# Split weights at a new place within their buffers for each feature-major projection: a float32 decoder kernel on one Trainium2 core

## The chip, the cores and the metric

The kernel runs on one core of one Trainium2 chip. The metric is the device time of one execution in microseconds (us). The engines are named as the profile names them: PE is TensorE's matmul side and PEld its weight load, DVE is VectorE, ACT is ScalarE, POOL is GpSimd, SP is SyncE, which here only issues DMAs. SBUF is the on-chip memory in which each of 128 partitions holds its own row of bytes; PSUM is where matmuls accumulate.

## What is computed

The reference is a two-layer decoder over 256 positions of width 2048, in float32. Cut to its matrix products:

```python
# layer 0
z = rmsnorm(x, g_mix[0]) @ w_in_a[0]            # 2048 x 3584
x = x + concat([gating(z), memory_attention(z_q, mem)]) @ w_out[0]
x = x + conv_ffn(rmsnorm(x, g_ffn[0]), w_ffn_up[0], w_ffn_down[0])
# layer 1
kv = rmsnorm(x, g_kv) @ w_kv_a                  # 2048 x 576
z = rmsnorm(x, g_mix[1]) @ w_in_b[0]            # 2048 x 1024
x = x + concat([latent_attention(z, kv), memory_attention(z_q, mem)]) @ w_out[1]
x = x + conv_ffn(rmsnorm(x, g_ffn[1]), w_ffn_up[1], w_ffn_down[1])
out = rmsnorm(x, g_final)
```

`conv_ffn` is `(silu(gate) * val) @ w_down` with `[gate, val] = conv3(h @ w_up)`; `w_up` is 2048 x 11264 and `w_down` 5632 x 2048, so the two feed-forward blocks hold most of the work. `memory_attention` also projects 256 memory tokens with `w_mem_kv` (2048 x 1024 in each layer).

## The kernel before, in words

Every weight is read once from HBM and used once, for 256 positions. To keep float32 accuracy, weights and activations are each split into a high and a low part of type float32r (a rounded float32 of 4 bytes), and a product is made of three parts: high by high, high by low, low by high.

**Weights.** `chunk` (L92) fetches one piece of a weight matrix, normally 128 x 1024 floats (512 KB), with a DMA that SP issues into a buffer `raw` (L98). ACT rounds it into `whi` (L117, or L122 where a gain is multiplied in), and DVE subtracts to get `wlo` (L118, or L123). Each of `raw`, `whi` and `wlo` has four buffers of 4096 bytes in a partition. In the compiled program they follow one another without a gap; every one of the twelve starts at a byte that is 96 modulo 256.

**Feature-major projections.** `gemm_fm` (L158) makes 512 columns of the output (`nblk` = 4 blocks of 128) or 256 (`nblk` = 2). The weights are the stationary operand: each matmul first loads 128 columns of `whi` or `wlo` (512 bytes in a partition) and then streams the activation. An activation operand is `[high 256 | low 256]`, so one matmul with `whi` streams 512 columns (L140, a "high" matmul below), and one with `wlo` streams the 256 high columns (L144, a "low" matmul). `mm_fm` (L135) issues the high and the low matmuls of two chunks in runs, and turns the order round at every second call, so that runs of 32 high and 32 low matmuls come about. The results are evicted by `join` (L220) and the code of each stage. The calls with `nblk` = 4, in the program's order, are: the keys of the memory of layer 0 and of layer 1; in layer 0 four groups of `w_in_a`, four of `w_out`, 22 of `w_ffn_up` and 12 of `w_ffn_down`; in layer 1 the latent key, the latent query and the memory query, four of `w_out` and 22 of `w_ffn_up`. That is 73 calls. `keys` (L809) calls `gemm_fm` with `nblk` = 2; `queries` (L795) and the rotary key (L764 to L766) call `chunk` and `mm_fm` themselves.

**Token-major projections.** `gemm_tm` (L187) has the activations stationary and streams 512 columns of weights: `whi` (L182), `wlo` (L183) and `whi` once more (L184). It makes the values of the memory in both layers, three groups of `w_in_a`, the values of the latent attention, and the down projection of layer 1.

**Order.** The instructions' order on each engine comes from a planner that is given the program; only a stretch of the last projection is written out by hand. A buffer's next use waits until its last reader is done: `whi` for the matmuls of four chunks earlier, `raw` for DVE, and the DMA for `raw`.

Of the kernel before, what the change touches and what calls it, by code (L numbers as in the profile page):

```python
# [9 lines left out]
F32R = mybir.dt.float32r  # L10
# [6 lines left out]
P = 128  # L17
# [13 lines left out]
THETA = 10000.0  # L31
EPS = 1e-6
FF_GROUPS = (4, 4, 3)


def exact_pieces(value, bits, count):
# [33 lines left out]
class Kernel:  # L70
    def __init__(self, ctx, tc, t, out):
        self.tc, self.nc, self.t, self.out = tc, tc.nc, t, out
        self.ctx = ctx
        self.n = 0
        pool = lambda name, bufs=1, **k: ctx.enter_context(tc.tile_pool(name=name, bufs=bufs, **k))
        self.cp = pool("cp")
        self.wp = pool("wp")
        self.ap = pool("ap")
        self.ps = pool("ps", 8, space=bass.MemoryType.PSUM)
# [12 lines left out]
    def chunk(self, src, nk, ncol, gains=None, twice=False, heads=None):  # L92
        nc, n = self.nc, nk * ncol
        raw = self.wp.tile([P, 1024], F32, tag="raw", name=self.uid("raw"), bufs=4)
        hi = self.wp.tile([P, 1024], F32R, tag="whi", name=self.uid("whi"), bufs=4)
        lo = self.wp.tile([P, 1024], F32R, tag="wlo", name=self.uid("wlo"), bufs=4)
        view = lambda x: x[:, :n].rearrange("p (k c) -> p k c", k=nk)
        nc.sync.dma_start(out=view(raw), in_=src)  # L98
        if twice:
            both = lambda x: x.rearrange("p (k o c) -> p k o c", o=2, c=ncol)  # L100
            for k in range(nk):
                s = slice(k * ncol, (k + 1) * ncol)
                for o in range(2):
                    h = both(hi)[:, k, o, :]
                    nc.scalar.activation(h, raw[:, s], AF.Copy, scale=gains[k])
                    nc.vector.scalar_tensor_tensor(both(lo)[:, k, o, :], raw[:, s], gains[k], h.bitcast(F32), ALU.mult, ALU.subtract)
            return tuple(x.rearrange("p (k c) -> p k c", k=nk) for x in (hi, lo))
        if heads is not None:

            s = view(raw).rearrange("p k (h c) -> p k h c", h=2)  # L110
            for c0, c1 in ((0, heads), (heads, ncol // 2)):
                o = lambda x: view(x)[:, :, 2 * c0 : 2 * c1].rearrange("p k (h c) -> p k h c", h=2)
                nc.scalar.activation(o(hi), s[:, :, :, c0:c1], AF.Copy)
                nc.vector.tensor_tensor(o(lo), s[:, :, :, c0:c1], o(hi).bitcast(F32), ALU.subtract)
            return view(hi), view(lo)
        if gains is None:
            nc.scalar.activation(hi[:, :n], raw[:, :n], AF.Copy)  # L117
            nc.vector.tensor_tensor(lo[:, :n], raw[:, :n], hi[:, :n].bitcast(F32), ALU.subtract)  # L118
        else:
            for k in range(nk):  # L120
                s = slice(k * ncol, (k + 1) * ncol)
                nc.scalar.activation(hi[:, s], raw[:, s], AF.Copy, scale=gains[k])  # L122
                nc.vector.scalar_tensor_tensor(  # L123
                    lo[:, s], raw[:, s], gains[k], hi[:, s].bitcast(F32), ALU.mult, ALU.subtract
                )
        return view(hi), view(lo)
# [29 lines left out]
            low(jobs)  # L156

    def gemm_fm(self, src, kbs, nblk, rhs, evict, nk=2, gain=None, hooks={}):  # L158
        accs = [self.psum() for _ in range(nblk)]
        chunks = list(range(0, len(kbs), nk))  # L160
        for c0 in range(0, len(chunks), 2):
            jobs = []
            for c in chunks[c0 : c0 + 2]:
                g = None if gain is None else [gain(kbs[c + i]) for i in range(nk)]
                hi, lo = self.chunk(src(kbs[c], nk), nk, nblk * P, g)
                for b in range(nblk):
                    cols = slice(b * P, (b + 1) * P)
                    for i in range(nk):
                        kk = c + i
                        jobs.append((accs[b], hi[:, i, cols], lo[:, i, cols], rhs(kbs[kk]), kk == 0, kk == len(kbs) - 1))  # L170
            self.mm_fm(jobs, (c0 // 2) % 2)
            for c in range(c0, min(c0 + 2, len(chunks))):
                for f in hooks.get(c, ()):
                    f()
        for b in range(nblk):
            evict(b, accs[b])
# [154 lines left out]
    def gain(self, name, k):  # L331
        c = self.g[name] + k
        return self.gT[:, c : c + 1]
# [224 lines left out]
    def ffn(self, l, after=None, to_tokens=None, tokens=None):  # L558
# [5 lines left out]
        with self.tc.tile_pool(name=self.uid("ff"), bufs=1) as fp:  # L564
            g0 = 0
            for part, ng in enumerate(FF_GROUPS):
                h = self.ap.tile([P, NB, 512], F32R, tag="big", name=self.uid("h"))
# [11 lines left out]
                for g in range(g0, g0 + ng):  # L579
# [15 lines left out]
                    self.gemm_fm(self.rows(up, FF + g * 512, 512), ks, 4, lambda k: xhl[:, k, :], ev, hooks=turns)  # L595
                last = part == len(FF_GROUPS) - 1
                if last and l == 0:
# [403 lines left out]
```

## Time and profile before

| | |
|---|---|
| median of 3 runs | 2127.53 us (2127.27 to 2128.79) |
| profiled execution, first to last instruction (span) | 2125.1 us |
| instructions | 31077 |
| mean granted TensorE clock | 0.998 |
| read from HBM | 387.88 MB, 184 GB/s over the span |
| time between issue and landing of a 512 KB weight DMA | about 4.2 us |

The page gives no time for the profiled execution other than its span; the median of the runs is 2.4 us longer than it. In the profile a matmul's or a weight load's duration is modelled and contains a fixed latency, and consecutive ones overlap, so their pace is read from starts, or from the length of a run of them divided by their number.

### The profile page before, as it was taken

Reading aid. Unit: us, or ns where it says so; the run is one execution under the profiler, and the core shown is the slowest. Engines: PE = TensorE matmul, PEld = TensorE weight load, DVE = VectorE, ACT = ScalarE, POOL = GpSimd, SP = SyncE. Lnnn points to the kernel's source line nnn. Section 1 sums busy time; section 2 is a strip of 40 time slices with the busy share of each in tenths; the row PEclk is TensorE's granted clock in tenths of the full one; section 3 lists DMA queues with packets and bytes.
Section 4 is the critical chain, followed back from the end, with each engine's and each line's share of the span. In section 5 each row is a group of like instructions: output and inputs, shape, how many; then the busy total and the mean of one; then the engine's idle time right before and its main releaser. Section 6 shows DMA issues by size and latency. Waiting matters only on the chain.

```text
span 2125.1 us, 31077 instructions
## 1 busy us (share of the span) xinstructions
PE 2101.5 (99%) x11624; PEld 1831.1 (86%) x11624; DVE 1465.7 (69%) x2186; ACT 1148.7 (54%) x1773; POOL 392.8 (18%) x378
## 2 busy tenths in 40 slices
PE   8999999999999999999999999999999999999998
PEld 7888888888888888888888788888888888888886
DVE  6655667777756777567798766677775577745775
ACT  7654654556535555356556554466553555535554
POOL 1000123312101121011254111332120121201210
PEclk9999999999999999999999999999999999999999
DMA  8565555666566665666655533665656666656664
GB/s 272 178 202 178 159 187 189 189 189 191 189 194 187 185 195 188 197 182 188 192 181 165 171 114 110 196 190 170 191 196 195 187 190 190 194 195 188 189 188 149
DMA packets 207548, 392.01 MB, mean 184 GB/s; under 512 B 14302, under 2 KB 22820, under 8 KB 207268
## 3 DMA queue, kind: packets, MB, share of 16 engines
q1 hardware_dynamic: 207252, 389.50, 59.3%
q8 instruction: 91, 1.49, 0.3%
q14 instruction: 61, 0.50, 0.1%
q10 hardware_dynamic: 144, 0.52, 0.1%
HBM read 387.88 MB, written 2.10 MB: 184 GB/s over the span
## 4 chain that ended last, share of the span: by engine, by line
PE 97%; DVE 1%; ACT 1%; DMA 1%; issue 0%; SPq 0%; DVEq 0%; ACTq 0%
PE ps L140 50%; PE ps L144 26%; PE ps L182 6%; PE ps L184 6%; PE ps L183 6%; PE ps L831 1%; DMA raw<-in_w_mem_kv 0%; PE ps L829 0%; PE ps L523 0%; PE ps L488 0%; DVE wlo L118 0%; PE ps L665 0%; PE ps L852 0%; DMA raw<-in_w_in_a 0%; PE ps L393 0%
## 5 line engine op out<-in xcount | busy, mean ns | idle before, releaser
L118 DVE TENSOR_TENSOR wlo<-raw,whi 128x1024 fp32r<-128x1024 f32 x660 | 843.1, 1288 | 490.3 <-ACT whi L117 362.4
L117 ACT ACTIVATE whi<-raw 128x1024 fp32r<-128x1024 f32 x660 | 697.2, 1058 | 702.7 <-PE ps L140 525.4
L140 PE MATMUL ps<-xhl,whi 128*128 128x512 f32 x3280 | 768.9, 390 | 0.0
L140 PEld LDWEIGHTS ps<-xhl,whi 128*128 128x128 f32 x3280 | 608.6, 188 | 121.7
L571 POOL TENSOR_TENSOR a<-js,rbc 128x256 f32<-128x256 f32 x176 | 230.5, 1323 | 1101.7 <-DVE js L224 1005.8
L144 PEld LDWEIGHTS ps<-xhl,wlo 128*128 128x128 f32 x3280 | 408.7, 192 | 9.2 <-DVE wlo L118 0.6
L144 PE MATMUL ps<-xhl,wlo 128*128 128x256 f32 x3280 | 413.4, 283 | 0.4 <-DVE wlo L118 0.4
L140 PE MATMUL ps<-h,whi 128*128 128x512 f32 x704 | 164.8, 390 | 0.0
L574 ACT ACTIVATE c<-a,cT 128x256 f32<-128x256 f32 x176 | 105.2, 598 | 96.9 <-POOL a L571 95.3
L140 PEld LDWEIGHTS ps<-h,whi 128*128 128x128 f32 x704 | 130.6, 188 | 26.0
L183 PE MATMUL ps<-wlo,h 128*128 128x512 f32 x352 | 136.8, 389 | 0.0
L182 PE MATMUL ps<-whi,h 128*128 128x512 f32 x352 | 136.6, 389 | 0.0
L184 PE MATMUL ps<-whi,h 128*128 128x512 f32 x352 | 136.3, 389 | 0.0
L140 PE MATMUL ps<-mainhl,whi 128*128 128x512 f32 x512 | 119.7, 390 | 0.0
L140 PEld LDWEIGHTS ps<-mainhl,whi 128*128 128x128 f32 x512 | 95.1, 188 | 19.1
L123 DVE SCALAR_TENSOR_TENSOR wlo<-raw,gT,whi 128x512 fp32r<-128x512 f32 x112 | 87.9, 829 | 25.2 <-ACT whi L122 23.0
L576 DVE SCALAR_TENSOR_TENSOR c<-a,cT,c 128x254 f32<-128x254 f32 x176 | 101.1, 587 | 0.0
L575 DVE SCALAR_TENSOR_TENSOR c<-a,cT,c 128x255 f32<-128x255 f32 x176 | 91.6, 539 | 11.6 <-ACT c L574 11.4
L122 ACT ACTIVATE whi<-raw,gT 128x512 fp32r<-128x512 f32 x112 | 74.7, 716 | 42.3 <-PE ps L140 20.0
L224 DVE TENSOR_TENSOR js<-ps,cr 128x256 f32<-128x256 f32 x213 | 84.1, 417 | 12.6 <-POOL a L571 12.3
L222 ACT ACTIVATE cr<-ps 128x256 f32<-128x256 f32 x243 | 79.4, 373 | 19.7 <-PE ps L140 16.5
L144 PEld LDWEIGHTS ps<-h,wlo 128*128 128x128 f32 x704 | 87.7, 191 | 2.0
(248 smaller groups left out, 1856.2 us busy)
## 6 DMA issues: line engine op xcount, KB each, us to landing
raw<-in_w_ffn_up SPq DMA_DIRECT2D x352, 512.0 KB, 4.2
raw<-in_w_ffn_down SPq DMA_DIRECT2D x176, 512.0 KB, 4.4
raw<-in_w_out SPq DMA_DIRECT2D x64, 512.0 KB, 4.1
raw<-in_w_in_a SPq DMA_DIRECT2D x56, 512.0 KB, 4.1
raw<-in_w_mem_kv SPq DMA_DIRECT2D x32, 512.0 KB, 4.8
raw<-in_w_in_b SPq DMA_DIRECT2D x16, 512.0 KB, 3.9
raw<-in_w_uq SPq DMA_DIRECT2D x12, 384.0 KB, 3.3
raw<-in_w_kv_a SPq DMA_DIRECT2D x8, 512.0 KB, 4.2
```

Of the source, the lines that this page charges most:

```text
L117: nc.scalar.activation(hi[:, :n], raw[:, :n], AF.Copy)
L118: nc.vector.tensor_tensor(lo[:, :n], raw[:, :n], hi[:, :n].bitcast(F32), ALU.subtract)
L123: nc.vector.scalar_tensor_tensor(lo[:, s], raw[:, s], gains[k], hi[:, s].bitcast(F32), ALU.mult, ALU.subtract)
L140: mm(acc[:, :], wh, x, start=first, stop=last)
L144: mm(acc[:, S:], wl, x[:, :S], start=False, stop=False)
L182: mm(acc, xh, wh, start=first, stop=False)
L183: mm(acc, xh, wl, start=False, stop=False)
L184: mm(acc, xl, wh, start=False, stop=last)
L571: nc.gpsimd.tensor_tensor(a, self.join(acc), rb, ALU.mult)
L574: nc.scalar.activation(c, a, AF.Identity, scale=w(2), bias=w(3))
L575: nc.vector.scalar_tensor_tensor(c[:, 1:], a[:, : S - 1], w(1), c[:, 1:], ALU.mult, ALU.add)
L576: nc.vector.scalar_tensor_tensor(c[:, 2:], a[:, : S - 2], w(0), c[:, 2:], ALU.mult, ALU.add)
```

## The change

`hi` and `lo` become windows of 1024 floats in buffers that are 64 floats (256 bytes) longer. A counter `place` gives the start of the window. It starts at 0 and goes up by one at each call of `gemm_fm` with `nblk` = 4, modulo 64. All other users of `chunk` take the place that the counter has at that time. `raw` stays where it is in its buffer. To make room, 12 KB of a reserve at the start of SBUF, which is kept for DMA descriptors that software writes, are given up. The new buffers are 4352 bytes, and all other tiles move by multiples of 256 bytes, so place p puts a weight's start at byte (96 + 4p) modulo 256, and everything else keeps its address modulo 256.

```diff
+PLACES = 64
...
+        self.place = 0
...
-        hi = self.wp.tile([P, 1024], F32R, tag="whi", name=self.uid("whi"), bufs=4)
-        lo = self.wp.tile([P, 1024], F32R, tag="wlo", name=self.uid("wlo"), bufs=4)
+        hi = self.wp.tile([P, 1024 + PLACES], F32R, tag="whi", name=self.uid("whi"), bufs=4)
+        lo = self.wp.tile([P, 1024 + PLACES], F32R, tag="wlo", name=self.uid("wlo"), bufs=4)
+        hi, lo = (x[:, self.place : self.place + 1024] for x in (hi, lo))
...
     def gemm_fm(self, src, kbs, nblk, rhs, evict, nk=2, gain=None, hooks={}):
+        if nblk == 4:
+            self.place = (self.place + 1) % PLACES
...
-    nc = bacc.Bacc("TRN2", target_bir_lowering=False, num_devices=1)
+    nc = bacc.Bacc("TRN2", target_bir_lowering=False, num_devices=1, dynamic_dma_scratch_size=4096)
```

Counting the 73 calls gives the place of each stage: 1 and 2 for the memory's keys (and with them its values), 2 for the token-major groups of `w_in_a`, 3 to 6 for the other groups of `w_in_a`, 7 to 10 for `w_out`, 11 to 44 for the feed-forward block of layer 0 (its down projection at 19 to 22, 31 to 34 and 41 to 44), 45 to 47 for the projections of layer 1 (the rotary key at 46; values, queries and keys at 47), 48 to 51 for `w_out`, 52 to 63 and 0 to 9 for the up projections of layer 1. The three parts of its down projection, which is token-major, lie at 59, 3 and 9.

## The prediction

> **What bounds the kernel now.** I read the page first: busy times, the 40 slices, the chain of work that ended last.
>
> ```profile
> PE 2101.5 (99%) x11624; PEld 1831.1 (86%) x11624; DVE 1465.7 (69%) x2186; ACT 1148.7 (54%) x1773; POOL 392.8 (18%) x378
> ...
> PE   8999999999999999999999999999999999999998
> ...
> PEclk9999999999999999999999999999999999999999
> ```
>
> ```profile
> PE 97%; DVE 1%; ACT 1%; DMA 1%; issue 0%; SPq 0%; DVEq 0%; ACTq 0%
> ```
>
> PE is busy in every slice at the full clock, and 97% of the chain that sets the end is PE. Busy time alone can't say whether PE runs at its pace, since its durations are modelled. So next comes the chain in order of time, in a window inside the first feed-forward block (start, length, what):
>
> ```profile
> 399.90 0.36 PE ps L144 x3
> 400.26 7.28 PE ps L140 x32
> 407.54 3.83 PE ps L144 x32
> 411.38 7.28 PE ps L140 x32
> 418.66 3.83 PE ps L144 x32
> 422.49 0.69 PE ps L140 x3
> ```
>
> Each run starts where the one before ends: there is no gap. A high matmul (512 columns) takes 7.28 / 32 = 227.5 ns, a low one (256 columns) 3.83 / 32 = 119.7 ns. The difference, 107.8 ns for 256 columns, gives 0.421 ns a column, so either kind has a fixed 119.7 - 107.8 = 11.9 ns beside its columns. The same chain in the token-major down projection of layer 1:
>
> ```profile
> 1584.88 0.23 PE ps L183
> 1585.10 0.23 PE ps L184
> ...
> 1586.92 0.23 PE ps L183
> ```
>
> Nine matmuls lie between the first start and the last: 2.04 / 9 = 226.7 ns. How many there are says the view of busy time by stretch, taken over the whole span for L140, L144, L182, L183 and L184 in turn; its bracketed counts are matmuls and weight loads:
>
> ```profile
> 0.00:2126.00 2126.00, 1118.07 (x4744) 880.18 (x4744) 1.00 0.60 184
> 0.00:2126.00 2126.00, 598.33 (x4744) 591.98 (x4744) 1.00 0.60 184
> 0.00:2126.00 2126.00, 210.04 (x536) 101.11 (x536) 1.00 0.60 184
> 0.00:2126.00 2126.00, 209.22 (x536) 101.20 (x536) 1.00 0.60 184
> 0.00:2126.00 2126.00, 208.83 (x536) 101.03 (x536) 1.00 0.60 184
> ```
>
> 4744 x 0.2275 + 4744 x 0.1197 + 1608 x 0.2267 = 1079 + 568 + 365 = 2012 us of a span of 2125.1. The other 113 us are the start, the attention and the end. **The kernel is bound by the pace of its float32r matmuls**, and the question is whether that pace depends on the byte at which a weight starts.
>
> **The change part by part.** *What it adds and removes.* No matmul, activation, subtraction or DMA comes or goes, and no wait: each still depends on the same buffers, of which there are as many. Choosing a window costs nothing at run time. The reserve that is given up serves descriptors written by software, and the page's list of DMA queues has no such queue; the weights come over this one:
>
> ```profile
> q1 hardware_dynamic: 207252, 389.50, 59.3%
> ```
>
> This part is 0.
>
> *ACT and DVE.* They now write `whi` and `wlo`, and DVE reads `whi`, at a place that is a multiple of 4 bytes but mostly of nothing larger. Their groups before:
>
> ```profile
> L118 DVE TENSOR_TENSOR wlo<-raw,whi 128x1024 fp32r<-128x1024 f32 x660 | 843.1, 1288 | 490.3 <-ACT whi L117 362.4
> L117 ACT ACTIVATE whi<-raw 128x1024 fp32r<-128x1024 f32 x660 | 697.2, 1058 | 702.7 <-PE ps L140 525.4
> ```
>
> The trace has an operation at such places already. L575 and L576 read and write `c` from its second and third column on, 4 and 8 bytes past its start; L235 is the same DVE operation with everything at the tile's start. From the views of these lines (shortest/median/longest ns):
>
> ```profile
> L575 DVE SCALAR_TENSOR_TENSOR c<-a,cT,c x176: 468/477/957, 396.6 to 2061.3; 128x255 f32<-128x255 f32 x176
> ```
>
> ```profile
> L576 DVE SCALAR_TENSOR_TENSOR c<-a,cT,c x176: 465/478/968, 397.4 to 2063.5; 128x254 f32<-128x254 f32 x176
> ```
>
> ```profile
> L235 DVE SCALAR_TENSOR_TENSOR chl<-ck,gT,chl x4: 473/475/477, 1168.1 to 1169.3; 128x256 fp32r<-128x256 f32 x4
> ```
>
> 477 and 478 ns against 475: a shift of one or two words costs DVE nothing for 256 columns, within 3 ns. So L118 should keep its time. ACT has no shifted operation in the trace; I bound it by room. Eight high and eight low matmuls consume a chunk, (7.28 + 3.83) / 4 = 2.78 us, and L117 takes 1.06 of them. ACT is busy 54% and DVE 69% of the time, so ACT's share in a chunk could grow by about 1.28 us and DVE's by 0.86 us before PE would wait. Below that bound it is hidden by PE; I take 0 on the path. Were that cover gone, as it would be if both took twice as long (DVE 1.3 us more against 0.86 of room), 0.4 us in each of L118's 660 chunks would come out, about 0.28 ms; the DVE rows speak against it.
>
> *PE, stationary side.* In the feature-major projections the shifted weights are what PE loads, 128 columns at a time. A load goes beside the matmul ahead of it. How fast a load can follow a load shows in the attention, where float32 matmuls of 128 columns come in pairs, each with a load of its own:
>
> ```profile
> 1232.35 0.39 PE L862 MATMUL ps<-pT,scratch 128*128 128x128 f32 x2
> 1232.58 0.39 PE L863 MATMUL ps<-pT,scratch 128*128 128x128 f32 x2
> 1232.80 0.39 PE L861 MATMUL ps<-pT,scratch 128*128 128x128 f32 x2
> 1233.02 0.39 PE L862 MATMUL ps<-pT,scratch 128*128 128x128 f32 x2
> ```
>
> 0.67 us for six loads: 111 ns each. Against a high matmul's 227.5 ns a load has 116 ns to spare, against a low one's 119.7 only 9. So a slower load shows in the low matmuls first, and from 9 ns on. That float32 loads and float32r loads are alike is not shown; if a float32r load is what makes a low matmul last 119.7 ns, there is nothing to spare. The two ends are therefore 0 (no dependence on the place, or less than 9 ns) and what the second and third rivals below price. I take 0, since it is nearest to the one kind of row that has a shift, L575 and L576: there 4-byte places are as fast as others.
>
> *PE, moving side.* In the token-major projections all 1608 matmuls stream the shifted weights at 0.421 ns a column, and nothing hides a slower stream. No row has a shifted moving operand; the bounds are again 0 and the rivals' prices, and I take 0 by the same rows.
>
> *Sum.* 0 + 0 + 0 + 0 on a span of 2125.1 us. The median of the runs is 2.4 us longer, so **the forecast is 2127.5 us**, and no change means 2123.3 to 2131.8 (0.2%, about what a measurement of this kernel can tell).
>
> **The rivals.** *1. Crossing lines (slower, small).* If PE fetches in lines of some bytes, a weight that starts inside a line touches one line more. With lines of 16 bytes, 4 columns, places that are multiples of 4 are free: 18 of the 73 calls, 1136 of the low matmuls (64 a call, 48 in call 44), which leaves 4744 - 1136 = 3608. If the load sets the low matmul's pace, a line more costs 4 x 119.7 / 128 = 3.7 ns: 13.5 us. The token-major places 1, 2, 47, 59, 3 and 9 are all off the lines: 1608 x 4 x 0.421 ns = 2.7 us. Together 2127.5 + 16.2 = **2143.7 us**. With the load hidden in its 9 ns only 2130.2 is left; with lines of 32 bytes some 7/8 of the low matmuls pay 7.5 ns and the token-major ones 3.4: 31 + 5, 2164. For it: nothing in the trace moves 512 bytes per partition to PE from an odd start, and the low matmuls have at most 9 ns of cover. Against it: the fixed 11.9 ns can swallow a first line, and DVE's rows show no such step. [...]
>
> *2. A pair of words on the moving side (slower, large).* PE streams float32r at 0.421 ns a column. The L862 row's matmul of plain float32 takes 111 ns for 128 columns, about twice that for a column. So float32r is read at double pace, perhaps as pairs of words. If a pair must start at a multiple of 8 bytes, odd places stream at half pace. Odd are 1, 47, 59, 3 and 9: 96 + 72 + 1056 = 1224 matmuls, each 512 x 0.421 = 215.6 ns longer: +264, **2391 us**; if three steps do for two pairs, half of it, 2259. For it: the double pace. Against it: only that other engines don't mind. It decides from one odd place on; half price still stands out.
>
> *3. The same on the stationary side (slower, large).* A load of 111 ns at half pace takes 222, with the 11.9 behind it 234: a low matmul gets 114 ns longer, a high one 6.5. 37 of the 73 calls have odd places, and values and keys of the attention as well: 35 x 64 + 2 x 48 + 120 = 2456 pairs, +296, **2423 us**. A load takes 111 / 128 = 0.87 ns a column, single pace, so pairs are less likely here.
>
> *4. The present place is a bad one (faster).* 96 modulo 256 is no multiple of 64. If the fixed 11.9 ns came from that, five calls (places 8, 24, 40, 56 and 8 again) of 64 low matmuls would save 3.8 us: **2123.7**. If every other place were free of it, 4744 x 11.9 ns, 56 us, is the bound. Nothing speaks for it but that the 11.9 ns is unexplained.
>
> That the change doesn't do what it says is hardly open: the place enters every weight's address. A planner that orders otherwise is the last case, with no sign or price.
>
> **How the numbers follow.** No change 0.52; rival 1 0.24; rival 2 0.12; rival 3 0.06; rival 4 0.05; another order 0.01. The likeliest is 2127.5. The range takes no change, all of rival 1 up to 2164 and the likelier part (0.04) of rival 4: **2121 to 2166**, 0.80; rivals 2 and 3 stay outside. Of rival 1, 0.04 lies within 0.2% (its 2130 end), of rival 4 0.01. Same: 0.52 + 0.04 + 0.01 = 0.57. Slower: 0.20 + 0.12 + 0.06 + 0.01 = 0.39. Faster: 0.04.
>
> **What would show it.** Right: runs of 32 high and 32 low matmuls keep 7.28 and 3.83 us in every stage, at odd places and even ones, and the down projection of layer 1 its 0.227 us. Rival 1 shows as 3.83 growing by 0.1 us or more except at places 12, 16, 20 and so on; rival 2 as about 0.44 us per matmul after 1560 us alone; rival 3 as low runs near 7.5 us in every second call. L118 and L117 should keep their means of 1288 and 1058 ns; if they grow by over half and waits of PE on `wlo` appear, my account of ACT and DVE is wrong. A pace that differs with the place, in whichever direction, is what would make the forecast wrong.

## The result, and the profile after

The changed kernel takes 2146.39 us (median of 4 runs, 2146.14 to 2147.49) against 2127.40 before (4 runs, 2127.09 to 2128.79): ratio 1.0088, 95% interval 1.0074 to 1.0103. It is slower by 19 us, or 0.9%, where no change was forecast. The time lies inside the range that was given, close to the 2143.7 us of the rival "crossing lines". That it lies there is luck: the range reached so far up for that rival alone, and the rival turns out to have the wrong mechanism.

The page of the changed kernel first: the busy line, the granted clock, and the groups of weights and matmuls. Its lines have moved: L143 is L140 of before (high), L147 is L144 (low), L187 to L189 are L182 to L184, L121 is L118, and L120 is L117.

```profile
span 2145.8 us, 31077 instructions
PE 2122.8 (99%) x11624; PEld 1826.3 (85%) x11624; DVE 1467.3 (68%) x2186; ACT 1149.9 (54%) x1773; POOL 392.0 (18%) x378
...
PEclk9999999999999999999999999999999999999999
...
PE 97%; ACT 1%; DMA 1%; DVE 1%; issue 0%; SPq 0%; ACTq 0%
...
L121 DVE TENSOR_TENSOR wlo<-raw,whi 128x1024 fp32r<-128x1024 f32 x660 | 843.1, 1288 | 507.0 <-ACT whi L120 370.5
L120 ACT ACTIVATE whi<-raw 128x1024 fp32r<-128x1024 f32 x660 | 699.0, 1060 | 722.2 <-PE ps L143 525.6
```

As many instructions, the same clock, the same share of PE in the chain. DVE's subtraction keeps its 1288 ns to the digit, and ACT's rounding goes from 1058 to 1060. On the mean of all the places ACT and DVE keep their times within 2 ns. So the time went into PE itself. Its busy time over the span for L143, L147, L187, L188 and L189, in the view of busy time by stretch (behind the length: PE, then PEld):

```profile
0.00:2146.00 2146.00, 1140.29 (x4744) 881.07 (x4744) 1.00 0.60 183
0.00:2146.00 2146.00, 590.86 (x4744) 584.81 (x4744) 1.00 0.60 183
0.00:2146.00 2146.00, 211.62 (x536) 101.22 (x536) 1.00 0.60 183
0.00:2146.00 2146.00, 210.97 (x536) 101.61 (x536) 1.00 0.60 183
0.00:2146.00 2146.00, 210.23 (x536) 101.28 (x536) 1.00 0.60 183
```

Against the rows of before, the high matmuls take 1140.3 - 1118.1 = 22.2 us more and the low ones 598.3 - 590.9 = 7.5 us *less*. In the token-major stages the three lines overlap one another, so there I add the distances between starts: 371.8 us before, 377.5 after, 5.7 more. Together 20.4 of the 20.7 us by which the span grew. Some matmuls became slower, others faster, and no gap appeared between them.

How that looks in the chain in order of time, at three places of the feed-forward blocks: place 16, then place 30, then place 0 (start, length, what).

```profile
492.16 3.63 PE ps L147 x32
495.79 7.46 PE ps L143 x32
503.25 3.63 PE ps L147 x32
```

```profile
806.16 3.81 PE ps L147 x32
809.97 7.26 PE ps L143 x32
817.22 3.81 PE ps L147 x32
```

```profile
1764.85 7.28 PE ps L143 x32
1772.13 3.83 PE ps L147 x32
```

At place 0 stand the 7.28 and 3.83 us of before. At place 16 the high run is longer by 0.18 us and the low run shorter by 0.20. At place 30 both are about as before. Behind the first few matmuls of a run the distances between starts repeat in a pattern: in the high run at place 16 they are 231 and 236 ns in turn, in the low run 113 or 114. So what can be compared is their mean. Worked out from all the starts, from the seventh matmul of a run on, in ns between starts:

| place | bytes past the activations' start | high | low |
|---|---|---|---|
| every call before; 0 | 0 | 226.7 | 120.0 |
| 7 | 28 | 228.8 | 116.6 |
| 8 | 32 | 233.3 | 118.2 |
| 16 | 64 | 233.1 | 113.3 |
| 22 | 88 | 233.3 | 113.3 |
| 30 | 120 | 226.7 | 119.3 |
| 40 | 160 | 233.3 | 119.9 |
| 53 | 212 | 236.6 | 117.3 |

Places 1 to 9 come twice, in the first 360 us and near the end. Seven of them give the same two numbers within 0.3 ns both times; place 3 differs by 2.8 ns in high, place 6 by 1.8 in low. So the pace belongs mostly to the place, and not to chance or to the stage. The mean over the 73 calls is 232.1 for high and 118.2 for low. And the weights at place 40 start at byte 0 modulo 256, the roundest address there is, yet their high matmuls are among the slower ones.

### The profile page after: what moved, and what is told of

The parts are those of the page before. It is cut to its first block, busy times and chain, and to the rows that moved or that the text cites. A ratio compares the mean times of both kernels' runs of the same rounds, so it can differ in the third digit from the quotient of the medians.

```text
span 2145.8 us, 31077 instructions
## 1 busy us (share of the span) xinstructions
PE 2122.8 (99%) x11624; PEld 1826.3 (85%) x11624; DVE 1467.3 (68%) x2186; ACT 1149.9 (54%) x1773; POOL 392.0 (18%) x378
## 4 chain that ended last, share of the span: by engine, by line
PE 97%; ACT 1%; DMA 1%; DVE 1%; issue 0%; SPq 0%; ACTq 0%
PE ps L143 51%; PE ps L147 26%; PE ps L187 6%; PE ps L188 6%; PE ps L189 6%; PE ps L836 1%; PE ps L834 0%; PE ps L528 0%; DMA mtok<-in_mem 0%; PE ps L493 0%; DMA raw<-in_w_mem_kv 0%; PE ps L670 0%; ACT junk L410 0%; PE ps L857 0%; DMA raw<-in_w_in_a 0%
## 5 line engine op out<-in xcount | busy, mean ns | idle before, releaser
L121 DVE TENSOR_TENSOR wlo<-raw,whi 128x1024 fp32r<-128x1024 f32 x660 | 843.1, 1288 | 507.0 <-ACT whi L120 370.5
L120 ACT ACTIVATE whi<-raw 128x1024 fp32r<-128x1024 f32 x660 | 699.0, 1060 | 722.2 <-PE ps L143 525.6
L143 PE MATMUL ps<-xhl,whi 128*128 128x512 f32 x3280 | 783.6, 395 | 0.0
L143 PEld LDWEIGHTS ps<-xhl,whi 128*128 128x128 f32 x3280 | 608.8, 188 | 134.8
L576 POOL TENSOR_TENSOR a<-js,rbc 128x256 f32<-128x256 f32 x176 | 229.6, 1316 | 1114.4 <-DVE js L229 1018.4
L147 PEld LDWEIGHTS ps<-xhl,wlo 128*128 128x128 f32 x3280 | 404.4, 188 | 10.3 <-DVE wlo L121 0.6
L147 PE MATMUL ps<-xhl,wlo 128*128 128x256 f32 x3280 | 408.9, 281 | 0.4 <-DVE wlo L121 0.4
L143 PE MATMUL ps<-h,whi 128*128 128x512 f32 x704 | 168.5, 395 | 0.0
L143 PEld LDWEIGHTS ps<-h,whi 128*128 128x128 f32 x704 | 130.6, 188 | 29.3
L188 PE MATMUL ps<-wlo,h 128*128 128x512 f32 x352 | 137.9, 392 | 0.0
L187 PE MATMUL ps<-whi,h 128*128 128x512 f32 x352 | 137.8, 392 | 0.0
L189 PE MATMUL ps<-whi,h 128*128 128x512 f32 x352 | 137.1, 391 | 0.0
L143 PE MATMUL ps<-mainhl,whi 128*128 128x512 f32 x512 | 121.8, 394 | 0.0
L143 PEld LDWEIGHTS ps<-mainhl,whi 128*128 128x128 f32 x512 | 95.0, 188 | 21.1
L147 PEld LDWEIGHTS ps<-h,wlo 128*128 128x128 f32 x704 | 86.2, 188 | 2.3
```

Source lines behind the costliest of these rows:

```text
L143: mm(acc[:, :], wh, x, start=first, stop=last)
L147: mm(acc[:, S:], wl, x[:, :S], start=False, stop=False)
L187: mm(acc, xh, wh, start=first, stop=False)
L188: mm(acc, xh, wl, start=False, stop=False)
L189: mm(acc, xl, wh, start=False, stop=last)
L576: nc.gpsimd.tensor_tensor(a, self.join(acc), rb, ALU.mult)
```

## The experiments

**Theory.** The second column of the table is what counts: the distance between the start of the weights that PE loads and the start of the activations that it streams at the same time. Loads run beside matmuls: before, PEld is busy for 1831.1 us and PE for 2101.5 of a span of 2125.1, so at least 1807.5 us of the loads fall into the time of matmuls. My guess is that the two reads from SBUF, one for the next matmul and one for the present one, get in each other's way or don't, depending on how their addresses lie to one another. **Rivals:** the weight's own address counts (lines, pairs of words); the writes of ACT and DVE into the weight buffers disturb PE; the longer buffers, the smaller reserve, or the change from place to place cost something.

The ratios below are to executions of the kernel before that were taken beside each experiment; their medians are 2126.29 to 2126.88 us.

### Is it the place, its address, or a distance?

*frozen0*: the counter stays at 0, all else of the change is kept.

```diff
     def gemm_fm(...):
-        if nblk == 4:
-            self.place = (self.place + 1) % PLACES
```

> The changed kernel with its counter left at 0: longer buffers and the smaller reserve stay, every weight starts at 96 modulo 256 as before. If the place alone costs the 19 us (my theory): 2127.4 us, high matmuls at 226.7 ns, low ones at 120.0. Rival (buffer length or the reserve has a part in it): above 2129.

Measured: 2126.92 us, ratio 1.0001 (0.9991 to 1.0011). The buffers and the reserve have no part in it.

*all32*: the kernel before, and everything in SBUF lies 32 bytes further on.

```diff
-    nc = bacc.Bacc(..., num_devices=1)
+    nc = bacc.Bacc(..., num_devices=1, dynamic_dma_scratch_size=16384 + 32)
```

> The kernel before with everything in SBUF 32 bytes further on, so that weights and activations both start at 128 modulo 256. Theory (the distance between the start of the weights that are loaded and that of the activations that are streamed sets the pace): the distance is 0 as before, 2127.4 us, runs of 32 at 7.28 and 3.83 us. Rival (the weight's own place counts, lines or the like): as place 8 in the changed kernel, high 233.3 and low 118.2 ns, 4744 x (6.6 - 1.8) ns = 23 us more, about 2150.

Measured: 2126.23 us, ratio 1.000 (0.9991 to 1.0010).

*acts32*: the kernel before, with a small tile ahead of the activations, which moves them and not the weights.

```diff
+        self.pad = self.ap.tile([P, 8], F32, name="pad")
+        nc.vector.memset(self.pad, 0.0)
         self.x = self.ap.tile([P, NB, S], F32, name="xT")
```

> The kernel before with all activation operands 32 bytes further on; raw, whi and wlo stay at 96 modulo 256, so ACT and DVE write the weights where they did. Theory (distance): weights lie 32 bytes, or 224 modulo 256, from the activations as at place 56, high 233.5 and low 116.7 ns: 4744 x (6.8 - 3.3) = 17 us more, and up to 10 more in the token-major stages, 2144 to 2154. Rivals (the weight's own place; or ACT's and DVE's writes of the weights getting in PE's way): 2127.4.

Measured: 2149.37 us, ratio 1.0108 (1.0093 to 1.0123).

*frozen8*: as frozen0, with `self.place = 8`.

> The changed kernel with its counter held at 8: every weight starts at 128 modulo 256, a multiple of 64, the activations at 96. Theory (distance, here 32 bytes): high 233.3 and low 118.2 ns in every stage, 4744 x (6.6 - 1.8) = 23 us, and 0 to 10 in the token-major stages: 2150 to 2160. Rival (lines of 64 bytes or less, of which a start at 128 crosses none more): 2127.4 or below. Rival (it is the change from place to place that costs): 2127.4.

Measured: 2155.24 us, ratio 1.0136 (1.0121 to 1.0151).

These four are read together. The same stretch of the chain in all32, acts32 and frozen8, in this order:

```profile
413.50 7.28 PE ps L140 x32
420.78 3.83 PE ps L144 x32
```

```profile
404.70 7.47 PE ps L140 x32
412.17 3.74 PE ps L144 x32
415.91 7.47 PE ps L140 x32
423.37 3.77 PE ps L144 x32
```

```profile
401.87 3.79 PE ps L147 x32
405.66 7.46 PE ps L143 x32
413.13 3.79 PE ps L147 x32
416.92 7.46 PE ps L143 x32
```

In all32 and in frozen8 the weights start at the same byte, 128 modulo 256. With the activations there too, the runs are those of before; with the activations 32 bytes earlier, the high runs take 7.46. In acts32 the weights are where they always were, and only the streamed side moved: 7.47. A start at a multiple of 64 bytes costs 29 us in frozen8, and nothing in all32. So between these two addresses the weight's own place decides nothing, and no rule on it alone, by lines or by pairs of words, can give both times.

That it is the distance shows in the paces. Worked out as for the table, acts32 has 233.3 (high) and 117.0 ns (low) on the mean of the calls; place 56 of the changed kernel, 224 bytes past the activations' start and so at the same distance modulo 256, has 233.5 and 116.7. frozen8 has 233.4 and 118.2, place 8 has 233.3 and 118.2. In the token-major down projection of layer 1, where PE loads the activations and streams the weights, acts32 and frozen8 both take 233.3 ns a matmul against 226.7 before.

frozen8 also gives no sign that the other engines' traffic has a part. Its two low runs above, 3.79 us each, in the view by stretch (PE, PEld, DVE, ACT and POOL busy):

```profile
401.87:405.66 3.79, 3.79 (x34) 3.79 (x33) 3.79 (x7) 3.65 (x6) 1.93 (x2) 1.00 0.60 154
413.13:416.92 3.79, 3.79 (x33) 3.79 (x33) 2.36 (x2) 1.06 (x1) 0.00 (x0) 1.00 0.61 150
```

In the first DVE works all the time and ACT nearly so, in the second 62% and 28% of it, with POOL idle. The length is the same. The DMA's share hardly differs between the two, so of that this pair says nothing.

### High and low apart

*hi_only* and *lo_only*: the places for one of the two buffers alone. For hi_only:

```diff
-        hi, lo = (x[:, self.place : self.place + 1024] for x in (hi, lo))
+        hi, lo = hi[:, self.place : self.place + 1024], lo[:, :1024]
```

> The changed kernel with the places for whi alone; wlo stays at 96 modulo 256. Theory (each matmul's pace follows from the distance between the weights loaded beside it and the activations, high and low apart): high as in the changed kernel, +22 us, low at 120.0 as before, token-major +2 to 6: 2150 to 2156, slower than the changed kernel. Rival (one loss from the change from one kind of run to the other): near 2137.

Measured: 2154.30 us, ratio 1.0135 (1.0118 to 1.0152). High takes 1137.74 us of busy time (+19.7 over before), low 597.57 (-0.8), and the token-major stages 7.7 us more by their starts, 2 above the expected range. High and low are separate to within 3 us (with both places high took 22.2 more), and without the low matmuls' gain the time is worse than with the whole change.

> The changed kernel with the places for wlo alone; whi stays at 96 modulo 256. Theory: high at 226.7 as before, low at 118.3 on the mean, -7 us, token-major 0 to +3: 2119 to 2124, faster than before. Rival (any place other than the activations' costs): above 2130.

Measured: 2130.42 us, ratio 1.0017 (1.0008 to 1.0027): slower, not faster. That is the time of the rival, but not its reason: the low matmuls became faster at the new places. The feature-major part came out about as expected: low takes 592.21 us of busy time, 6.1 less than before, high 2.1 more. The miss is in the token-major stages, which took 8.2 us more by their starts where 0 to 3 was expected: in layer 1's down projection 232.2 ns a matmul against 226.7. There `whi` and `wlo` are streamed alternately and now lie at different distances from the activations. By the starts, the two matmuls of each three that stream `whi`, whose addresses are those of before, take 234.5 and 232.8 ns there, and the one that streams `wlo` takes 229.4. So the loss isn't confined to the matmuls whose operand moved; it looks as if what happens beside one matmul is carried into the next. The next section shows the same more plainly.

### The better place for the low weights

From the table, low weights at place 16 or 22 and high ones at place 0 should give the best of both columns. *lo16* and *lo22* put `wlo` there in the feature-major projections, and leave it at 96 in the others (shown for 16):

```diff
-        hi, lo = (x[:, self.place : self.place + 1024] for x in (hi, lo))
+        hi, lo = hi[:, :1024], lo[:, self.place : self.place + 1024]
...
-        if nblk == 4:
-            self.place = (self.place + 1) % PLACES
+        self.place = 16 if nblk == 4 else 0
...
+        self.place = 0
         for b in range(nblk):
             evict(b, accs[b])
```

> whi at 96 modulo 256 throughout; wlo at place 16 (160 modulo 256, 64 bytes past the activations' start) in the feature-major projections, at 96 elsewhere. Theory: high 226.7, low 113.3 ns as at place 16 in the changed kernel: 4608 x 6.67 ns = 31 us less, 2094 to 2098. Rival (113.3 needs the high runs of place 16 ahead of it, to enter in step): low 118 to 120, 2117 to 2127.

Measured: 2117.94 us, ratio 0.9963 (0.9948 to 0.9978).

> As the kernel with wlo at place 16, with place 22 instead (184 modulo 256, 88 bytes past the activations' start, not a multiple of 16). Theory: the low matmuls keep the 113.3 ns that place 22 had in the changed kernel, 2094 to 2098; a distance needs no round number. Rival (only multiples of 64 bytes suit): 2117 to 2127.

Measured: 2102.37 us, ratio 0.9888 (0.9873 to 0.9903). The chain of lo16, then of lo22:

```profile
406.60 3.77 PE ps L147 x32
410.37 7.28 PE ps L143 x32
```

```profile
405.99 3.65 PE ps L147 x32
409.64 7.28 PE ps L143 x32
```

At place 16 the low matmuls come at 117.8 ns, not at the 113.3 they had in the changed kernel: the rival named beside the expectation is right here. At place 22 they do come at 113.3. The time misses the expected 2094 to 2098 by some 5 us, because the first matmuls of each run take longer: a run of 32 lasts 3.65 us against 3.83 before, a gain of 0.18 and not of 32 x 6.67 ns = 0.21, and the 4608 low matmuls make 144 such runs. In the memory query of layer 1 two other matmuls break into a run of low ones, and behind them the low ones come at 115 to 121 ns. Over the whole span the low matmuls of lo22 are busy

```profile
0.00:2156.00 2156.00, 573.11 (x4744) 568.02 (x4744) 1.00 0.58 182
```

that is 25.2 us less than the 598.33 of before, which is the 24 us that the kernel gained.

*both16* asks whether the run before decides: `whi` and `wlo` both at place 16 in the feature-major projections. Against lo16:

```diff
-        hi, lo = hi[:, :1024], lo[:, self.place : self.place + 1024]
+        hi, lo = (x[:, self.place : self.place + 1024] for x in (hi, lo))
```

> whi and wlo at place 16 in the feature-major projections, 96 modulo 256 elsewhere. If the state in which a run of low matmuls is entered decides (wlo at 16 with whi at 96 gave 117.8 ns, with whi at 16 in the changed kernel 113.3): high 233.1, low 113.3, 4608 x (6.4 - 6.7) ns, near 2126. Rival (113.3 at place 16 was chance of one call): low 117 to 118, 2145 to 2150.

Measured: 2124.88 us, ratio 0.9991 (0.9981 to 1.0000).

```profile
408.19 3.63 PE ps L147 x32
411.82 7.46 PE ps L143 x32
419.28 3.63 PE ps L147 x32
```

The low runs are back at 3.63 in this stretch, and at 113.3 ns within 0.3 in 62 of the 73 calls (114.3 to 116.8 in the others), now that the high runs beside them go at 7.46. The others mix two paces. The latent key of layer 1 has both in one call, with the same places and the same kernel:

```profile
1107.07 3.63 PE ps L147 x32
1110.70 4.89 PE ps L143 x21
1115.59 0.43 PE ps L259 x2
1116.02 2.57 PE ps L143 x11
1118.59 3.77 PE ps L147 x32
```

Two matmuls of a normalization (L259) break into the high run, and the low run behind it lasts 3.77 us, as in lo16, and not 3.63. So for the same distance there is more than one pace, 3.63 or 3.77 us for a run of 32 here, and which of them a run had went with the high run ahead of it. At place 22 the good pace is reached behind high runs at place 22 (the changed kernel) and behind high runs at place 0 (lo22).

### How far the pattern goes, and which access counts

*lo86*: lo22 with `wlo` another 256 bytes further on (`PLACES = 128`, place 86).

> wlo at place 86, which is 256 bytes past place 22, with buffers of 1152 floats; whi at 96 modulo 256. Theory with a period of 256 bytes: low 113.3 ns, time as the kernel with wlo at place 22, 2100 to 2105. Rival (more address bits count): another low pace, 2106 to 2127.

Measured: 2100.92 us, ratio 0.9881 (0.9866 to 0.9896), low runs 3.65 us. As far as this one distance shows, 256 bytes more change nothing.

*read22*: DVE writes `wlo` where it always did, and only PE's window is shifted. Against lo22:

```diff
-        hi, lo = hi[:, :1024], lo[:, self.place : self.place + 1024]
+        hi, shifted, lo = hi[:, :1024], lo[:, self.place : self.place + 1024], lo
+        if self.place:
+            nc.gpsimd.memset(lo[:, 1024 : 1024 + self.place].bitcast(F32), 0.0)
+        lo = lo[:, :1024]
...
-        return view(hi), view(lo)
+        return view(hi), view(shifted)
```

> DVE writes wlo at 96 modulo 256 as before, but PE loads its weights from a window 88 bytes further on (place 22); POOL fills the last 22 floats with zeros, so the low product uses weights shifted by 22 columns. Theory (only PE's own two reads count, load and stream): low 113.3 ns as with wlo written there, 2100 to 2106. Rival (where DVE writes counts): low 120, 2125 to 2130.

Measured: 2100.54 us, ratio 0.9878 (0.9864 to 0.9893).

```profile
407.98 7.28 PE ps L146 x32
415.26 3.65 PE ps L150 x32
```

At this place the window that PE reads sets the pace; where DVE writes does not.

## Why the prediction was wrong

**What bounds the kernel** stood: PE's pace in runs without gaps carried 20.4 of the 20.7 us by which the span grew.

**ACT and DVE, buffers, reserve at 0** stood: 1288 and 1060 ns after, and frozen0 at ratio 1.0001.

**The step that failed is "PE, stationary side" and "PE, moving side": "I take 0, since it is nearest to the one kind of row that has a shift, L575 and L576".** Those rows are DVE's. That DVE reads and writes at 4-byte places without loss held, with 1288 ns for its subtraction before and after, and it says nothing of PE, where a load runs beside a stream: in the two stretches of frozen8 above, PE and PEld are both busy for all of the 3.79 us. The bounds I gave looked at one stream at a time, as if a load or a stream had a cost of its own at an address. What the runs showed is a cost of the pair: all32 and frozen8 have the same weight address and differ by 29 us. The terms that were put at 0 measured +22.2 us (high), -7.5 (low) and +5.7 (token-major).

**The cover of the load** was misread. I gave a load 116 ns to spare beside a high matmul and at most 9 beside a low one, and so expected any loss in the low matmuls first. It came in the high ones. Spare time for the load did not cover it: the high matmuls took 22.2 us more. Whether the load or the stream is held up, the runs don't show.

**The "fixed 11.9 ns"** was a wrong reading of two numbers. The best low pace is 113.3 ns and the best high pace 226.7, exactly twice: 0.443 ns a column, as if there were nothing beside it. The 119.7 of before was a low pace that was already 6 ns too slow. That hid in the difference of 107.8 which I took for the price of 256 columns.

**Rival 1, crossing lines**, gave 2143.7 and the measurement was 2146.4, but it is refuted. It has the loss in the low matmuls, which became faster. It has places 12, 16 and 20 free, and place 16 costs 6.4 ns in every high matmul. A start at 128 modulo 256 should be free, and frozen8 is the slowest of all kernels here. The DVE rows that I held against it could not speak of it: L575 and L576 start 4 and 8 bytes into a tile and end with it, so they would touch no line more than a whole row does. That PE fetches in lines of some size was an assumption of mine, and so was the price of a line; no run here shows either. What the runs showed in its place: lo22 loads its low weights at 184 modulo 256, a place that the rival charges for, and a low run lasts 3.65 us, while at 96, which the rival has free, it lasted 3.83. **Rivals 2 and 3, pairs of words**, fall as well: no token-major stage came near 0.44 us, and no low run near 7.5 us. The latest token-major part, at place 9, took 234.9 ns a matmul instead of 226.7.

**Rival 4, the present place is a bad one**, had 0.05 and a bound of 56 us. Its reason (96 is no multiple of 64) is wrong, since all32, at 128, has the same runs of 7.28 and 3.83 us. But its core, that the fixed part of a low matmul comes from where things lie, is what lo22 shows: 24 us to gain, of the 31 that 6.7 ns in each of 4608 matmuls would be.

What stays open: where in SBUF or PE the two reads meet, if they do, and why a distance has more than one steady pace. The runs show that distance and entry decide, and, at place 22, that 256 bytes more and the place of DVE's writes make no difference; they don't show the mechanism inside.

## What to carry to other kernels

Where matmuls run without gaps and each loads its weights beside the stream of the one before, the distance between the two operands' starts in a partition can be a parameter worth a few per cent: here the same program took from 2100.9 (lo86) to 2155.2 us (frozen8) with only operands moved. It is read from the lengths of runs of equal matmuls, high and low or wide and narrow apart, or from the busy time of one line, and not from PE's share of busy time, which is 99% in both kernels. A row of another engine was no evidence for PE here (DVE kept its 1288 ns where the high matmuls took 22.2 us more), and the place that is best in one sequence need not be so in another (16 gave 113.3 ns in the changed kernel and 117.8 in lo16), so it has to be tried with the sequence that will run.

## What the runs showed of the hardware that was not expected

- PE's pace depends on how the start of what it loads lies to the start of what it streams. In the changed kernel 512 columns took 226.7 to 236.6 ns and 256 columns 113.3 to 120.7 ns on the mean of a call, with no change in any instruction but its start address, in steps as fine as 4 bytes (place 0: 226.7 and 120.0; place 1, first call: 232.6 and 118.2).
- The two kinds want different things: equal starts are best for 512 columns (226.7) and nearly the worst for 256 (120.0).
- The pace locks: within a run the distances between starts repeat in a pattern for tens of matmuls (231 and 236 ns in turn in the high runs at place 16), and the same distance locked at 113.3 or 117.8 ns depending on the run before it (both16 and lo16, and both within one call of both16).
